# Two-layer hybrid encoder trunk on one core: which FFN blocks are computed by seven products, which chunks they pair, and where the norm factors live

## The chip, the cores and the metric

The kernel runs on one core of one Trainium2 chip. The core has five engines, each with its own list of instructions: TensorE (PE, matmuls, with the loading of its stationary operand shown apart as PEld), VectorE (DVE), ScalarE (ACT), GpSimd (POOL) and SyncE (SP), which here issues most DMA transfers; some others are issued by POOL. An instruction starts when its engine reaches it and the semaphores that it waits for have been raised. The metric is the device time of one launch in microseconds, the median of several runs.

## What is computed

Two layers over 512 tokens of width 1024 in float32: three token mixers whose outputs are gated and merged, an output projection, a SwiGLU FFN of inner width 2816, and a gated embedding; every sublayer starts with an RMS norm. Cut to what the change touches:

```python
def rmsnorm(x, g):
    x32 = x.astype(jnp.float32)
    y = x32 * lax.rsqrt(jnp.mean(x32 * x32, axis=-1, keepdims=True) + EPS)
    return (y * g.astype(jnp.float32)).astype(x.dtype)
...
    for i in range(DEPTH):
...
        merged = (ga * (ya @ w_br_a[i]) + gb * (yb @ w_br_b[i])
                  + gc * (yc @ w_br_c[i]))
        x = x + merged @ w_o[i]
        h = rmsnorm(x, norm_ffn[i])
        x = x + (jax.nn.silu(h @ w_ffn_gate[i]) * (h @ w_ffn_up[i])) @ w_ffn_down[i]
        h = rmsnorm(x, norm_ple[i])
        x = x + jax.nn.sigmoid(h @ w_ple_gate[i]) * (p[i] @ w_ple_in[i])
    return rmsnorm(x, norm_final)
```

## The kernel before

*Layout.* Activations lie transposed: the 1024 features are 8 chunks of 128 partitions, each chunk 512 tokens wide. The 2816 inner features are 22 blocks of 128. The host lays each weight out by blocks of 128 output features, [128, 1024], in which column group k holds the weights of input chunk k.

*Float32 from halves.* Each operand is split in two: `split` (line 161) makes a high half on ACT (L142, rounded to fp32r) and the rest, the low half, on DVE (L156). A product is three matmuls, high times high, high times low and low times high (`mm3`, L176 to L178). `weights` (line 165) loads a block of weights on SP's queue and splits it.

*Norms.* A norm's factor is a number for each token, so it is taken out of the product: `norm_chunk` puts h = x times gain into a tile and sums the squares; `norm` turns the sums by PE (L212), reduces them on DVE (L214), takes the root on POOL (L221), and spreads the factors over the partitions with four transposes (L225) whose result `spread` copies into a tile of tag "r". `rows` then sets `self.rb`, by which later results are multiplied. Work that needs it waits in `ready`.

*Order.* PE's list is written out by hand. For the other engines a scheduler places the instructions by priority; `weights` and the preparation within `seven` run at a priority raised by `w_ahead` = 400 places, and `behind` ties one instruction after another by hand. Tiles come from pools by tag: a tag with n buffers can hold n tiles, and a new tile waits until the last reader of the one that it replaces is done.

*The stages around the change, in one layer.* The differential stage (its rotary tables are two tiles of tag "r", its norm at about 249 us); the merge, in which chunk m of `merged` is accumulated in `gatec_x` and split into halves (`merge_b`, tiles `mergeb_y` and `mergeb_v`); the output projection `w_o` from about 456 us in the first layer, whose first two output chunks are a `pair` (line 193): chunks 0 to 6 of the input for both outputs, then chunk 7 for both; then `main_norm` and the FFN. The FFN goes in three parts (`PARTS`, blocks 0 to 7, 8 to 14, 15 to 21), each with its up and gate blocks and then a down projection.

*A block of the FFN.* The plain way: `gemm` (block 0: `pair`) for the gate and for the up product, 2 x 8 x 3 = 48 matmuls of 512 columns. The other way, `seven` (blocks 3 to 21): with input chunks j and j + 4 as rows and the two halves of the tokens as columns, the activations are 2 x 2 matrices b11, b12, b21, b22; the weights of the two products form a 2 x 2 matrix as well, and the four results come from seven products over four pairs j, thus 7 x 4 x 3 = 84 matmuls of 256 columns. The sums of the activations, t1 to t4 for each j, are made once a layer by `quarters` (line 909), two sets within `w_o` after chunks 5 and 6, two in the FFN after blocks 0 and 1. The sums of the weights, s1 to s4, are made for each block: s1 and s2 by a load on SP's queue and an accumulating DMA from POOL (L953) on top of it, s3 = s1 + a22 and s4 = s3 + a12 on DVE (L967, L971, which show as L156); a22 is loaded into a tile of tag "r" (`ffn_r`) and split into "kh" and "a". The tiles s1 to s4 lie in tag "qk" (`ffn_qk`).

Of the kernel before, what the change touches and what calls it, by code (L numbers as in the profile page):

```python
# [12 lines left out]
F32R = mybir.dt.float32r  # L13
# [7 lines left out]
P = 128  # L21
L = 2
# [3 lines left out]
D = 1024  # L26
KD = 8
# [11 lines left out]
NFB = DFF // P  # L39
# [9 lines left out]
BG = dict(glu=2, natten=1, values=3, diff=1, gatec=2, branchc=2, gateb=4, mergea=4, mergea2=2)  # L49
FIRST = (["v"] * 4 + ["pt"] * 2 + ["y", "b"], ["y"] * 5 + ["pt"] * 2 + ["b"])  # L50
EARLY = 6
SEVEN = tuple(range(3, 22))
GAP = 144
BACC = dict(dynamic_dma_scratch_size=1024)

# [5 lines left out]
class Net:  # L61
# [189 lines left out]
        self.run(self.norm(sq, D, waits, self.rows))  # L251

    def spread(self, bc):
        r = self.sb("r", [P, 512])
        self.act(r, bc, AF.Copy)
        return r

# [32 lines left out]
    def build(self):  # L290
        nc, tc, a = self.nc, self.tc, self.a
        self.bufs = dict(wr=3, wh=3, wl=3, h=8, qk=2, kh=2, v=4, pt=2, y=5, z=5, x=4, t=7, rp=4,
                         e=4, a=3, r=3, ss=1, sm=8, rc=4, b=2, s=8)
        self.bg, self.w_ahead = BG, 400
        self.pbufs = dict(mm=3, sc=2, tr=2, av=1)
        with tc.tile_pool(name="sb", bufs=1) as self.pool, \
                tc.tile_pool(name="ps", bufs=1, space=PSUM) as self.psum, \
                tc.tile_pool(name="dr", bufs=1, space=DRAM) as dram:
            xs = dram.tile([KD, P, 512], F32, name="xs")
            self.pis = dram.tile([KD, P, 512], F32, name="pis")  # L300
            with tc.manual_schedule(engines={mybir.EngineType.PE}):
                h = self.opening()
                xsrc = a["xT"]
                for i in range(L):
                    h = self.layer(i, h, xsrc, xs)
                    xsrc = xs
# [578 lines left out]
    def w_o(self, mg, xsrc):  # L885
        self.phase = "wo"
        xs, h, st, self.four = [], [], [], []
        for m in range(KD):
            if m % 2 == 0:
                two = self.parts_of("x", [512], 2)  # L890
            xo = two[m % 2]
            self.nc.sync.dma_start(xo, xsrc[m])
            if m == 0:
                both = [self.ps("mm") for _ in range(2)]
                self.pair(both, self.a["w_o"][self.i, 0:2], mg)
            if m < 2:
                ps = both[m]
            else:
                ps = self.ps("mm")
                self.gemm(ps, self.a["w_o"][self.i, m], mg)  # L900
            self.tt(xo, xo, ps, ALU.add)
            h.append(self.norm_chunk(m, xo, self.par(self.i, "ffn", m), "h", st))
            xs.append(xo)
            if m in (5, 6):
                self.four.append(self.quarters(xs, h, m - 5))
        self.main_norm(st[0])
        return xs, h

    def quarters(self, x, h, j):


        one, two = slice(0, 256), slice(256, 512)
        g = lambda k: self.par(self.i, "ffn", k)
        f = []
        for k in (j, j + 4):
            v = self.sb("t", [P, 512])
            self.act(v, x[k], AF.Copy, scale=g(k))
            f.append(v)
        b11, b12, b21, b22 = f[0][:, one], f[0][:, two], f[1][:, one], f[1][:, two]
        u = self.sb("t", [P, 2, 256])  # L920
        w = self.sb("t", [P, 2, 256])
        t1, t2, t3, t4 = u[:, 0], u[:, 1], w[:, 0], w[:, 1]
        self.tt(t1, b11, b12, ALU.subtract)
        self.tt(t2, b22, t1, ALU.add)
        self.tt(t3, b22, b12, ALU.subtract)
        self.tt(t4, t2, b21, ALU.subtract)
        if j < 2:
            d = [self.sb("rp" if n < 2 else "e", [P, 2, 256], F32R) for n in range(4)]
        else:
            d = [q for _ in range(2) for q in self.parts_of("v", [2, 256], 2, F32R)]  # L930
        for o, t in zip(d, (t1, t2, t3, t4)):
            self.split(o[:, 0], o[:, 1], t)
        ha, hb = self.halves(h[j]), self.halves(h[j + 4])
        cut = lambda p, c: (p[0][:, c], p[1][:, c])
        return dict(b11=cut(ha, one), b21=cut(hb, one), b22=cut(hb, two),
                    **{f"t{n + 1}": (o[:, 0], o[:, 1]) for n, o in enumerate(d)})
# [100 lines left out]
    def ffn(self, h, x):  # L1037
        self.phase = "ffn"
        i = self.i
        self.halfs, self.pending = 0, []  # L1040
        st, hn, bs = [], [], self.four
        spare = [[self.sb(t, [P, 1024], F32R) for _ in range(2)] for t in ("y", "pt")]
        self.sums, self.sevens = [t for _ in range(2) for t in self.parts_of("qk", [1024], 2)], 0
        for part in PARTS:
            mids = []
            for f, fb in enumerate(part):
                tags = (("mm", "mm", "mm"), ("sc", "sc", "av"))[fb % 2]
                md = self.sb("z" if f < 5 else "y", [P, 2, 512], F32R)
                mids.append(md)
                wg, wu = self.a["w_fg"][i, fb], self.a["w_fu"][i, fb]  # L1050
                if fb in SEVEN:
                    self.seven(wg, wu, bs, tags, spare[fb % 2], md, part[0] and f < 2)
                    continue
                g = self.sb("t", [P, 512])
                pg, pu = (self.ps(t) for t in tags[:2])
                if fb == 0:
                    self.pair((pg, pu), (wg, wu), h)
                else:
                    self.gemm(pg, wg, h)

                def gate(pg=pg, g=g):
                    self.tt(g, pg, self.rb, ALU.mult)
                    self.act(g, g, AF.Silu, table="silu")

                self.ready(gate)
                self.flush()
                if fb:
                    self.gemm(pu, wu, h)

                def up(pu=pu, g=g, md=md):  # L1070
                    self.tt(g, g, pu, ALU.mult)
                    self.split(md[:, 0, :], md[:, 1, :], g)

                self.ready(up)
                if fb in (0, 1):
                    self.four.append(self.quarters(x, h, 2 + fb))
            self.flush()
            down = [self.a["w_fd"][i, m][:, part[0] * P:(part[-1] + 1) * P] for m in range(KD)]
            two = [self.ps(("mm", "sc")[fb % 2 == 0]) for _ in range(2)]
            self.pair(two, down[:2], mids)  # L1080
            for m in range(KD):
                if m < 2:
                    ps = two[m]
                else:
                    ps = self.ps("mm")
                    self.gemm(ps, down[m], mids)
                d = self.sb("t", [P, 512])
                self.tt(d, ps, self.rb, ALU.mult)
                self.tt(x[m], x[m], d, ALU.add)
                if part is PARTS[-1]:  # L1090
                    if m in (0, 2):
                        qk = self.parts_of("qk", [2, 512], 2, F32R)
                    hn.append(self.norm_chunk(m, x[m], self.par(i, "ple", m),
                                              qk[m % 2] if m < 4 else "v", st))
        self.main_norm(st[0])
        return hn

# [189 lines left out]
        return None  # L1287


def _blocks(w):  # L1290
    k, m = w.shape[-2:]
    lead = w.shape[:-2]
    n = len(lead)
    w = w.reshape(*lead, k // P, P, m // P, P)
    w = w.transpose(*range(n), n + 2, n + 1, n, n + 3)
    return np.ascontiguousarray(w).reshape(*lead, m // P, P, (k // P) * P)
# [17 lines left out]
def _token_order():  # L1314
    t = np.arange(S)
    return (t % GR) * GW + t // GR
# [37 lines left out]
def _layout(v):  # L1354
    n = _token_order()
    f = {k: np.asarray(a) for k, a in v.items()}
    w_in = f["w_in"]
    par = []
    for i in range(L):
# [14 lines left out]
        "head": np.ascontiguousarray(np.concatenate([_cols(f["norm_mix"][0]), w_0[0, :, :P]], axis=1)),  # L1374
        "w_0": w_0,
        "w_in": _blocks(w_in),
        "w_va": _vblocks(w_in[:, :, OFF_VA:OFF_VA + 512]),
        "w_vc": _wide(w_in[:, :, OFF_VC:OFF_VC + 512]),
        "w_br_a": _blocks(f["w_br_a"]),
        "w_br_b": _blocks(f["w_br_b"]),  # L1380
        "w_br_c": _blocks(f["w_br_c"]),
        "w_o": _blocks(f["w_o"]),
        "w_fg": _blocks(f["w_ffn_gate"]),
        "w_fu": _blocks(f["w_ffn_up"]),
        "w_fd": _blocks(f["w_ffn_down"]),
        "w_pi": _blocks(f["w_ple_in"]),
        "w_pg": _blocks(f["w_ple_gate"]),
# [16 lines left out]
```

## Time and profile before

| what | value |
|---|---|
| median of 3 runs | 1789.35 us (1788.98 to 1789.88) |
| profiled execution, its own time | 1788.65 us |
| its span in the profile | 1786.9 us |
| mean granted TensorE clock | 0.999 |
| the first layer's FFN, 514 to 886 us: PE, DVE, ACT busy | 372.0, 281.5, 173.2 us |
| all DMA | 251.31 MB, 141 GB/s on the mean |

The span runs from the first to the last instruction that the profiler records; the time of an execution has about 1.75 us more around it. A page gives busy time by engine, a chain of waits followed back from the last instruction, and groups of instructions by line. An entry such as `L156 DVE TENSOR_TENSOR wo_x<-wo_x,wo_mm 128x512 f32<-128x512 f32 x2` is line 156 on DVE, writing a tile of tag "x" made in stage "wo". In a timeline the first two numbers are start and duration in us, and a bracket at the end gives the idle time ahead of the instruction and what ended it. Lines often are those of a helper, so a place is told by its tiles.

### The profile page before, as it was taken

What the parts mean: (1) busy time and instruction counts of PE and PEld (TensorE: products, weight loads), DVE (VectorE), ACT (ScalarE), POOL (GpSimd) and SP (SyncE); (2) the same over time, 40 slices, a digit from 0 to 9 for tenths busy, and PEclk for the clock granted to TensorE, in tenths of its full rate; (3) what the DMA queues carried; (4) which work ended last, traced back from release to release, by engine and by line L of the source; (5) the groups of instructions that cost most, each with busy time, mean ns of one, the idle gap of its engine ahead of it and who ended that gap; (6) DMA issues with size and microseconds to landing.
All of it is one profiled execution on the core that took longest, in us unless ns stands there. A gap on an engine that the chain in (4) does not pass through costs nothing.

```text
span 1786.9 us, 26874 instructions
## 1 busy us (share of the span) xinstructions
PE 1775.8 (99%) x9994; PEld 1554.5 (87%) x9994; DVE 1392.3 (78%) x2354; ACT 880.9 (49%) x1531; POOL 92.1 (5%) x134
## 2 busy tenths in 40 slices
PE   9999999999999999999999999999999999999998
PEld 7888888888889899998888888888888898989987
DVE  7877887997678587787776788889886775877776
ACT  5577555325465254454545765453355553534444
POOL 0000000000101011100000000000001010101000
PEclk9999999999999999999999999999999999999999
DMA  5666541334737366543447655323256473645332
GB/s 206 190 182 171 156 116 44 111 98 145 227 111 182 111 164 160 135 115 124 146 135 202 170 158 151 101 71 95 95 172 198 130 177 111 176 135 158 98 104 94
DMA packets 109907, 251.31 MB, mean 141 GB/s; under 512 B 14160, under 2 KB 18768, under 8 KB 109776
## 3 DMA queue, kind: packets, MB, share of 16 engines
q1 hardware_dynamic: 98112, 228.36, 41.6%
q0 software_dynamic: 10944, 19.93, 6.9%
q8 instruction: 79, 1.29, 0.3%
q10 hardware_dynamic: 720, 1.31, 0.2%
q14 instruction: 52, 0.43, 0.1%
HBM read 210.74 MB, written 7.34 MB: 122 GB/s over the span
## 4 chain that ended last, share of the span: by engine, by line
PE 96%; ACT 2%; DVE 1%; issue 0%; DMA 0%; POOLq 0%; DVEq 0%; ACTq 0%
PE ffn_mm L176 5%; PE ffn_mm L178 5%; PE ffn_mm L177 5%; PE ffn_mm L983 3%; PE ffn_mm L982 3%; PE ffn_mm L981 3%; PE ffn_sc L983 3%; PE ffn_sc L982 3%; PE ffn_sc L981 3%; PE mergea_mm L176 2%; PE mergea_mm L178 2%; PE mergea_mm L177 2%; PE diff_sc L783 2%; PE gatec_mm L176 2%; PE gatec_mm L177 2%; PE gatec_mm L178 2%
## 5 line engine op out<-in xcount | busy, mean ns | idle before, releaser
L159 DVE SCALAR_TENSOR_TENSOR conv_z<-glu_z,pre_par,conv_z 128x512 f32<-128x512 f32 x240 | 179.6, 748 | 3.3
L142 ACT ACTIVATE ffn_wh<-ffn_wr 128x1024 fp32r<-128x1024 f32 (+1 forms) x98 | 99.0, 1018 | 142.2 <-PE ffn_mm L177 103.5
L156 DVE TENSOR_TENSOR ffn_wl<-ffn_wr,ffn_wh 128x1024 fp32r<-128x1024 f32 (+1 forms) x98 | 114.7, 1177 | 15.8 <-ACT ffn_wh L142 15.1
L953 POOL DMA_DIRECT2D ffn_qk<-w_fu x76 | 67.4, 980 | 567.2 <-DMA ffn_qk<-w_fu 304.2
L156 DVE TENSOR_TENSOR ffn_t<-ffn_mm,wo_r 128x512 f32<-128x512 f32 (+1 forms) x66 | 40.6, 616 | 68.3 <-PE ffn_mm L178 68.3
L176 PE MATMUL ffn_mm<-ffn_z,ffn_wh 128*128 128x512 f32 x220 | 85.6, 389 | 0.0
L177 PE MATMUL ffn_mm<-ffn_z,ffn_wh 128*128 128x512 f32 x220 | 85.6, 389 | 0.0
L178 PE MATMUL ffn_mm<-ffn_z,ffn_wl 128*128 128x512 f32 x220 | 85.6, 389 | 0.0
L142 ACT ACTIVATE mergea_wh<-mergea_wr 128x1024 fp32r<-128x1024 f32 (+1 forms) x32 | 27.1, 846 | 96.8 <-PE mergea_mm L177 79.6
L142 ACT ACTIVATE ffn_wh<-ffn_qk 128x1024 fp32r<-128x1024 f32 x38 | 40.3, 1061 | 35.2 <-PE ffn_mm L177 17.1
L156 DVE TENSOR_TENSOR ffn_wl<-ffn_qk,ffn_wh 128x1024 fp32r<-128x1024 f32 x38 | 46.5, 1224 | 12.3 <-ACT ffn_wh L142 12.3
L156 DVE TENSOR_TENSOR ffn_t<-ffn_t,ffn_t 128x512 f32<-128x512 f32 (+1 forms) x50 | 30.8, 627 | 31.1 <-ACT ffn_t L142 30.3
L142 ACT ACTIVATE diff_a<-diff_sc,diff_s 128x512 f32<-128x512 f32 x32 | 22.0, 686 | 61.3 <-DVE diff_s L874 61.3
L178 PEld LDWEIGHTS ffn_mm<-ffn_z,ffn_wl 128*128 128x128 f32 x220 | 41.3, 188 | 8.6
L176 PEld LDWEIGHTS ffn_mm<-ffn_z,ffn_wh 128*128 128x128 f32 x220 | 41.3, 188 | 8.5
L177 PEld LDWEIGHTS ffn_mm<-ffn_z,ffn_wh 128*128 128x128 f32 x220 | 41.3, 188 | 8.4
L142 ACT ACTIVATE natten_wh<-natten_wr 128x1024 fp32r<-128x1024 f32 x24 | 25.4, 1058 | 41.5 <-PE natten_sc L650 14.2
L983 PE MATMUL ffn_sc<-wo_h,ffn_wl 128*128 128x256 f32 x160 | 45.3, 283 | 0.0
L982 PE MATMUL ffn_sc<-wo_h,ffn_wh 128*128 128x256 f32 x160 | 45.3, 283 | 0.0
L981 PE MATMUL ffn_sc<-wo_h,ffn_wh 128*128 128x256 f32 x160 | 45.3, 283 | 0.0
L874 DVE TENSOR_REDUCE diff_s<-diff_sc 128x1 f32<-128x512 f32 x64 | 42.1, 685 | 3.9 <-PE diff_sc L783 3.7
L983 PE MATMUL ffn_mm<-wo_h,ffn_wl 128*128 128x256 f32 x144 | 40.8, 283 | 0.0
(816 smaller groups left out, 6451.0 us busy)
## 6 DMA issues: line engine op xcount, KB each, us to landing
ffn_wr<-w_fg SPq DMA_DIRECT2D x44, 512.0 KB, 3.6
ffn_qk<-w_fu POOLq DMA_DIRECT2D x76, 256.0 KB, 5.6
ffn_wr<-w_fd SPq DMA_DIRECT2D x32, 448.0 KB, 3.8
ffn_qk<-w_fg SPq DMA_DIRECT2D x38, 256.0 KB, 3.9
ffn_qk<-w_fu SPq DMA_DIRECT2D x38, 256.0 KB, 4.3
ffn_r<-w_fu SPq DMA_DIRECT2D x38, 256.0 KB, 4.3
natten_wr<-w_in SPq DMA_DIRECT2D x16, 512.0 KB, 4.4
natten_b<-bias SPq DMA_DIRECT2D x32, 256.0 KB, 4.0
```

Of the source, the lines that this page charges most:

```text
L142: i = self.nc.scalar.activation(out, in_, func, **kw)
L156: return self.nc.vector.tensor_tensor(out, a, b, op)
L159: return self.nc.vector.scalar_tensor_tensor(out, a, s, b, op0, op1)
L176: mm(out, wh, ah, start=first, stop=False)
L177: mm(out, wh, al, start=False, stop=False)
L178: mm(out, wl, ah, start=False, stop=last)
L783: self.nc.tensor.matmul(out, st4[:, u, qs], st[:, ks], start=n == 0, stop=n == 1)
L874: nc.vector.tensor_reduce(out=m[:, u:u + 1], in_=sc, op=ALU.max, axis=AX.X, negate=True)
L953: nc.gpsimd.dma_start(q, wu[:, lo], accum_op=ALU.add)
L981: mm(out, wh[:, c], bh, start=first and k == 0, stop=False, skip_group_check=True)
L982: mm(out, wh[:, c], bl, start=False, stop=False, skip_group_check=True)
L983: mm(out, wl[:, c], bh, start=False, stop=k == 3, skip_group_check=True)
```

## The change

Five edits, all in effect together:

1. `SEVEN` is gone: in every layer all blocks but block 0 go by `seven`, blocks 1 and 2 too.
2. A pair is two neighbouring chunks, 2j and 2j + 1, where it was j and j + 4. Three sets of sums are made in `w_o`, after chunks 2, 4 and 6; the fourth stands in the FFN ahead of block 0's matmuls. The host orders the column groups of the gate and up weights to match (`_halves`), and block 0's pair takes the chunks in `ORDER`.
3. The sums of the third and fourth set lie in four "z" tiles taken at the start of `w_o`, where they lay in "v" tiles.
4. The FFN's eight mid tiles are taken once (four "v", one "z", three "y") where each part took up to five "z" and the rest "y"; the last four chunks of the next norm lie in "z" rather than "v".
5. The norm factors get tag "rb" with one buffer, and "r" goes from three buffers to two.

```diff
-SEVEN = tuple(range(3, 22))
+QUARTERS = (2, 4, 6)
+ORDER = (0, 2, 4, 6, 1, 3, 5, 7)
...
     def spread(self, bc):
-        r = self.sb("r", [P, 512])
+        r = self.sb("rb", [P, 512])
...
-                         e=4, a=3, r=3, ss=1, sm=8, rc=4, b=2, s=8)
+                         e=4, a=3, r=2, rb=1, ss=1, sm=8, rc=4, b=2, s=8)
...
     def w_o(self, mg, xsrc):
         self.phase = "wo"
         xs, h, st, self.four = [], [], [], []
+        self.zs = [self.parts_of("z", [2, 256], 2, F32R) for _ in range(4)]
...
-            if m in (5, 6):
-                self.four.append(self.quarters(xs, h, m - 5))
+            if m in QUARTERS:
+                self.four.append(self.quarters(xs, h, QUARTERS.index(m)))
...
-        for k in (j, j + 4):
+        for k in (2 * j, 2 * j + 1):
...
-            d = [q for _ in range(2) for q in self.parts_of("v", [2, 256], 2, F32R)]
+            d = [q for n in range(2) for q in self.zs[2 * j - 4 + n]]
...
-        ha, hb = self.halves(h[j]), self.halves(h[j + 4])
+        ha, hb = self.halves(h[2 * j]), self.halves(h[2 * j + 1])
...
+        md8 = [self.sb(t, [P, 2, 512], F32R) for t in ["v"] * 4 + ["z"] + ["y"] * 3]
...
-                md = self.sb("z" if f < 5 else "y", [P, 2, 512], F32R)
+                md = md8[f]
...
-                if fb in SEVEN:
+                if fb:
                     self.seven(wg, wu, bs, tags, spare[fb % 2], md, part[0] and f < 2)
                     continue
                 g = self.sb("t", [P, 512])
                 pg, pu = (self.ps(t) for t in tags[:2])
-                if fb == 0:
-                    self.pair((pg, pu), (wg, wu), h)
-                else:
-                    self.gemm(pg, wg, h)
+                for j in range(len(QUARTERS), 4):
+                    self.four.append(self.quarters(x, h, j))
+                self.pair((pg, pu), (wg, wu), [h[k] for k in ORDER])
...
-                self.flush()
-                if fb:
-                    self.gemm(pu, wu, h)
...
-                if fb in (0, 1):
-                    self.four.append(self.quarters(x, h, 2 + fb))
...
-                                              qk[m % 2] if m < 4 else "v", st))
+                                              qk[m % 2] if m < 4 else "z", st))
...
+def _halves(w):
+
+    b = _blocks(w).reshape(L, NFB, P, KD, P)
+    return np.ascontiguousarray(b[:, :, :, ORDER]).reshape(L, NFB, P, D)
...
-        "w_fg": _blocks(f["w_ffn_gate"]),
-        "w_fu": _blocks(f["w_ffn_up"]),
+        "w_fg": _halves(f["w_ffn_gate"]),
+        "w_fu": _halves(f["w_ffn_up"]),
```

## The prediction, made before the changed kernel ran

> **What bounds the kernel now.** I read the page's busy shares first, then its chain of waits, then busy time by stretch, and last the timeline at the places that the change touches.
>
> ```profile
> span 1786.9 us, 26874 instructions
> PE 1775.8 (99%) x9994; PEld 1554.5 (87%) x9994; DVE 1392.3 (78%) x2354; ACT 880.9 (49%) x1531; POOL 92.1 (5%) x134
> PE 96%; ACT 2%; DVE 1%; issue 0%; DMA 0%; POOLq 0%; DVEq 0%; ACTq 0%
> ```
>
> TensorE (PE) is busy 99% of the span and makes 96% of the chain that ended last. The time is therefore the length of the list of matmuls, plus every gap that an edit puts into it. The stretches of the first layer that matter, and one of sevens (770 to 780) for comparison:
>
> ```profile
> core 0: us, PE busy (x) PEld busy (x) DVE busy (x) ACT busy (x) POOL busy (x), PEclk, DMA share, GB/s
> 450.00:460.00 10.00, 10.00 (x46) 8.29 (x45) 8.33 (x11) 4.03 (x5) 1.94 (x2) 1.00 0.87 301
> 460.00:470.00 10.00, 10.00 (x46) 8.28 (x45) 5.57 (x7) 4.28 (x6) 2.15 (x3) 1.00 1.05 273
> 480.00:490.00 10.00, 10.00 (x46) 8.29 (x45) 6.30 (x9) 5.61 (x8) 0.00 (x0) 1.00 0.30 89
> 490.00:500.00 10.00, 10.00 (x46) 8.29 (x45) 10.00 (x23) 8.61 (x16) 0.00 (x0) 1.00 0.29 103
> 500.00:510.00 10.00, 10.00 (x49) 8.27 (x49) 3.20 (x6) 2.04 (x4) 1.03 (x1) 1.00 0.25 79
> 770.00:780.00 10.00, 10.00 (x86) 10.00 (x85) 8.94 (x16) 5.59 (x10) 0.00 (x0) 1.00 0.36 97
> ```
>
> PE is busy in all of them at a granted clock of 1.00. Two resources have no room in places: the DMA engines from 450 to 470 (0.87, then 1.05, which is all 16), and VectorE (DVE) from 490 to 500 and, nearly, within the sevens.
>
> **The change part by part.** *Blocks 1 and 2 by seven products.* In each layer two blocks of 48 matmuls of 512 columns become 84 matmuls of 256. The starts of block 2, of block 3 (the first seven now) and of block 4 are in the PE timeline:
>
> ```profile
> 520.06 0.39 PE L176 MATMUL ffn_mm<-wo_h,ffn_wh 128*128 128x512 f32 x1
> 530.71 0.39 PE L178 MATMUL ffn_mm<-wo_h,ffn_wl 128*128 128x512 f32 x1
> 530.94 0.28 PE L981 MATMUL ffn_sc<-wo_h,ffn_wh 128*128 128x256 f32 x1
> 541.01 0.28 PE L981 MATMUL ffn_mm<-wo_h,ffn_wh 128*128 128x256 f32 x1
> ```
>
> A plain block takes 530.94 - 520.06 = 10.88 us, a seven 541.01 - 530.94 = 10.07 us. (Per matmul that is 227 and 120 ns: 256 columns cost more than half of 512.) The saving is 0.81 us a block, and over four blocks 3.24 us. That is the whole gain the change can have, 0.18% of the time.
>
> *What the new sevens ask of others.* Each adds DVE and ScalarE (ACT) work; the stretch 770 to 780 shows that DVE at 8.94 of 10 still keeps PE busy. Its loads grow from 1.0 to 1.75 MB (512 KB and three times 256 KB on SP's queue, two accumulating ones of 256 KB on POOL's), under a DMA share of 0.25 to 0.30 between 480 and 510. I cost this at nothing; if DVE's 1.1 us of room in 10 were gone, each of four blocks would be late by what is missing.
>
> *Where the first seven's preparation lands.* This is the edit that matters. The preparation runs at raised priority, 400 places early, so with block 1 a seven it moves from block 2's time back into the output projection and beyond. In the built order of the changed program, VectorE's list at the start of that projection reads: accumulate merged chunk 7; then s3 = s1 + a22 of block 1, which waits for the first accumulating DMA of the stage (that which adds w_fu to s1); then the low half of merged chunk 7. Both layers have it. Before, that addition came first at 513.8:
>
> ```profile
> L156 DVE TENSOR_TENSOR ffn_qk<-ffn_qk,ffn_r x38: 684/687/690, 513.8 to 1673.3; 128x512 f32<-128x512 f32 x38
> ```
>
> and the stretch ran thus, with its counterpart in the second layer:
>
> ```profile
> 456.94 1.06 POOL L953 DMA_DIRECT2D ffn_qk<-w_fu  x1 [39.27 <-DMA wo_wr<-w_o]
> 456.95 0.69 DVE L156 TENSOR_TENSOR gatec_x<-gatec_x,gateb_v 128x512 f32<-128x512 f32 x1
> 458.34 0.69 DVE L156 TENSOR_TENSOR mergeb_v<-gatec_x,mergeb_v 128x512 fp32r<-128x512 f32 x1 [0.70 <-ACT mergeb_v L142]
> 463.33 0.39 PE L176 MATMUL wo_mm<-mergeb_v,wo_wh 128*128 128x512 f32 x1
> 463.55 0.39 PE L177 MATMUL wo_mm<-mergeb_v,wo_wh 128*128 128x512 f32 x1
> 464.21 1.37 DVE L156 TENSOR_TENSOR wo_x<-wo_x,wo_mm 128x512 f32<-128x512 f32 x2 [5.18 <-PE wo_mm L178]
> ...
> 1342.22 0.93 POOL L953 DMA_DIRECT2D ffn_qk<-w_fu  x1 [39.17 <-DVE wo_wl L156]
> 1348.93 0.39 PE L177 MATMUL wo_mm<-mergeb_v,wo_wh 128*128 128x512 f32 x1
> ```
>
> The low half of chunk 7 is made at 458.34, and PE first needs it at 463.55, in the second matmul of the pair's last chunk. There are 4.5 us of room, and DVE idles 5.18 us. Now the low half stands behind a DMA issued at 456.94. How long such a DMA takes, by the views of DMA issues over 456.5 to 457.2, over 1342 to 1342.5, over 458.3 to 458.9 (the stage's second), and over the whole span:
>
> ```profile
> ffn_qk<-w_fu POOLq DMA_DIRECT2D x1, 256.0 KB, 8.3
> ffn_qk<-w_fu POOLq DMA_DIRECT2D x1, 256.0 KB, 7.5
> ffn_qk<-w_fu POOLq DMA_DIRECT2D x1, 256.0 KB, 9.1
> ...
> ffn_qk<-w_fu POOLq DMA_DIRECT2D x76, 256.0 KB, 5.6
> ```
>
> First layer: it lands at 456.94 + 8.3 = 465.24; the addition holds DVE for 0.60 (456.35 to 456.95 is the step from one such operation to the next), the low half takes 0.69, so PE goes on at 466.53, 2.98 us late. Second layer: 1342.22 + 7.5 + 1.29 = 1351.01 against 1348.93, 2.08 us late. Together 5.06 us. The ends: with 5.6 us the waits are 0.28 and 0.18, with 9.1 us 3.78 and 3.68, so 0.46 to 7.46 us. I take the two rows themselves, because the queue ahead of that DMA hardly changes: in the built order the loads before it are the same up to 454, and then a load of 256 KB for block 2 takes the place of a residual load of 256 KB. Queued behind the waiting addition are the low half, then the residual additions of chunks 0 and 1, which wait for PE anyway; SP's queue stops too, since the load of block 3's a22 waits for the addition to free its buffer, but the residual and weight loads behind it are needed some 20 us later.
>
> A rule speaks to each half of this. The built order puts the addition ahead, and the Trainium skill, "TensorE: Matmul & The Clock Gate", section "Architectural detail: the array is 16× 32×32, not 1× 128×128", says that the queues of ACT and DVE are strictly first in, first out; no run here shows it yet, and if DVE could pass the addition by, the sum would lose its 5.06 us. The rows say 8.3 and 7.5 us for 256 KB; the Trainium skill, "DMA: Bandwidth & Descriptors", section "Anatomy of one DMA — SWDGE (gpsimd) path", fits 2.0 us plus bytes over 436,000 per us, an estimate of 2.6 us here; by that the DMA would land at 459.5, the wait would be nothing and the time 1786.1. Here the rows differ from the page, and I go by the rows.
>
> *Pairs of neighbouring chunks.* The number of sums is the same; three sets instead of two are made within the projection, the fourth at once after it. A set is eight DVE operations of 256 columns, 0.34 us apart, 2.7 us. The new first set, after chunk 4, falls into 480 to 490, where DVE has 3.7 us idle. The last set now stands ahead of the norm:
>
> ```profile
> L156 DVE TENSOR_TENSOR wo_t<-wo_t,wo_t x12: 422/426/429, 490.3 to 1382.4; 128x256 f32<-128x256 f32 x12
> ...
> 503.41 0.69 DVE L214 TENSOR_REDUCE wo_sm<-wo_tr 128x4 f32<-128x512 f32 x1 [1.99 <-PE wo_tr L212]
> 504.46 1.03 POOL L221 TENSOR_TENSOR wo_rc<-wo_sm,pre_power 128x4 f32<-128x4 f32 x1 [32.34 <-DVE wo_sm L217]
> 508.70 0.60 PE L225 MATMUL wo_tr<-pre_ident,wo_rc 128*128 128x128 f32 x4
> ```
>
> The norm's own factor is ready at 505.5 and needed at 508.70. DVE had 2 us idle ahead of the reduction, so 2.7 us more make it about 1 us late, and 2 us of room remain. Nothing.
>
> *A tile of their own for the norm factors.* It frees two buffers for a22 before the factors exist. So block 1's and block 2's a22 load right after the rotary tables' last use (the first table's last read is the DVE row), and ACT splits block 1's a22 ahead of the softmax work of the differential stage:
>
> ```profile
> 241.22 0.68 DVE L156 TENSOR_TENSOR diff_rp<-diff_rp,diff_r 128x512 f32<-128x512 f32 x1
> 245.00 1.04 ACT L142 ACTIVATE gatec_wh<-gatec_wr 128x1024 fp32r<-128x1024 f32 x1
> 247.09 0.59 ACT L142 ACTIVATE diff_ss<-diff_av 128x512 f32<-128x512 f32 x1
> 249.19 0.60 PE L212 MATMUL diff_tr<-pre_ident,diff_ss 128*128 128x128 f32 x4
> ...
> ffn_qk<-w_fg SPq DMA_DIRECT2D x1, 256.0 KB, 3.6
> ffn_r<-w_fu SPq DMA_DIRECT2D x38, 256.0 KB, 4.3
> ```
>
> Issued at 241.9 it lands at 245.5 (3.6 us) or 246.2 (4.3). The split takes 0.6, so what starts at 245.00 starts at 246.1 or 246.8. The squares then end at 248.8 or 249.5, against 249.19: nothing, or about 0.3 us a layer. I take nothing, and keep 0.6 for the range. The rotary tables are loaded earlier too, at places where the next load waits for a buffer; nothing.
>
> *The sum*, against the profiled execution: 1788.65 us, which is the span of 1786.9 and 1.75 around it. 1788.65 - 3.24 + 5.06 = 1790.47. The median of the runs, 1789.35, stands 0.70 above that execution, so the forecast is **1791.2 us**, 0.10% over the time before. From no change a measurement of this kernel can tell about 0.2%, 3.58 us, so this counts as no change.
>
> **The rivals.** *The wait is covered.* If the first accumulating DMA landed by 463.55 - 1.29 = 462.26 in the first layer, after 5.3 us, and after 5.4 in the second, the saving would be whole: 1789.35 - 3.24 = 1786.1. For it speaks the median of 5.6 us; against it the DMA share of 1.05 at just that place. It lies 0.3 us inside the bound of 0.2% (1785.8), and the three runs spread 0.9, so one time in four or so it would count as faster.
>
> *The wait is longer.* The loads of the first three sevens now follow each other without the residual loads between, and all share the 16 engines with the accumulating DMA. Price: 9.1 us in both layers, as the stage's second took, gives 7.46 - 3.24 = +4.22, or 1793.6; with 0.6 from the differential stage 1794.2. It decides the sign from waits of 3.24 + 3.58 = 6.82 us in sum, that is 0.9 us a layer more than the rows say. For it: the engines are full, and the second row of its kind took 9.1. Against: what stands ahead in the queue is the same.
>
> *The sevens run quicker than those seen.* At half of 227 ns a seven would take 9.5 us and the four save 5.4 us, and with a covered wait the time would be 1784.0. Against it: all of the seven quoted runs at 120 ns.
>
> **How the numbers follow.** Forecast 0.44, covered wait 0.18, longer wait 0.33, quicker sevens 0.05. Same takes the forecast and three quarters of the covered wait, 0.57; slower 0.33; faster 0.05 and a quarter of 0.18, 0.10. The range goes from 1785.7, which is the covered wait less the 0.4 us by which the quickest run lies under the median, to 1794.7, which is the upper bound of both unknown costs plus the 0.5 by which the slowest lies over it; left out are the quicker sevens and waits longer than any row shows.
>
> **What would show it.** Right: PE idle some 3 us and 2 us in the middle of the output projection's first pair, in both layers, put down to VectorE, with DVE's s3 addition ended by the accumulating DMA just before; blocks 1 and 2 at 10.07 us each. Wrong: no gap there (the DMA lands early, or the order on DVE doesn't hold), a gap at 249.19 or at 508.70 of the first layer, or sevens that leave PE idle in blocks 1 and 2.

## The result and the profile after

| | median | runs | from to |
|---|---|---|---|
| before | 1788.98 us | 15 | 1788.13 to 1789.88 |
| changed | 1793.96 us | 15 | 1789.47 to 1797.19 |

The ratio is 1.0028 (95% interval 1.002 to 1.0036): the changed kernel is slower by 0.28%, 5.0 us. Its runs also lie 7.7 us apart, where those of before lie 1.8 apart. The profiled execution took 1792.81 us, 4.16 more than that of before. From the page of the changed kernel, the span, the busy times and the chain by engine:

```profile
span 1791.0 us, 27255 instructions
PE 1774.5 (99%) x10138; PEld 1559.7 (87%) x10138; DVE 1410.6 (79%) x2394; ACT 891.6 (50%) x1551; POOL 99.3 (6%) x142
PE 91%; DVE 4%; DMA 2%; ACT 2%; issue 1%; SPq 0%; DVEq 0%; POOLq 0%; ACTq 0%
```

PE is busy for 1.3 us less than before and the span is 4.1 us longer, so time went into waiting; VectorE and DMA now have a share in the chain. The places where PE waits longest, in the view of waits (engine and line, what it waited for, us in total, times, longest):

```profile
PE wo_mm L178 <- DVE mergeb_v L157: 6.0, 2, 3.6
```

Two waits, one for each layer, at the output projection and for the tile of merged chunk 7. (Lines stand one or two further down than before: L176 to L178 are L177 to L179 now, L156 is L157.) VectorE's timeline of the first layer, then PE's:

```profile
456.99 0.69 DVE L157 TENSOR_TENSOR gatec_x<-gatec_x,gateb_v 128x512 f32<-128x512 f32 x1
465.96 0.69 DVE L157 TENSOR_TENSOR ffn_qk<-ffn_qk,ffn_r 128x512 f32<-128x512 f32 x1 [8.29 <-DMA ffn_qk<-w_fu]
466.57 0.69 DVE L157 TENSOR_TENSOR mergeb_v<-gatec_x,mergeb_v 128x512 fp32r<-128x512 f32 x1
...
463.37 0.39 PE L177 MATMUL wo_mm<-mergeb_v,wo_wh 128*128 128x512 f32 x1
467.31 0.50 PE L178 MATMUL wo_mm<-mergeb_v,wo_wh 128*128 128x512 f32 x1 [3.56 <-DVE mergeb_v L157]
467.65 0.39 PE L179 MATMUL wo_mm<-mergeb_v,wo_wl 128*128 128x512 f32 x1
```

The accumulate of chunk 7 is followed by the addition s3 (`ffn_qk<-ffn_qk,ffn_r`), which stands idle for 8.29 us until the accumulating DMA has landed, and the low half of chunk 7 comes behind it, at 466.57 instead of 458.34. The chain of waits through the same stretch ties the pieces together (start, duration, what):

```profile
457.27 8.67 DMA ffn_qk<-w_fu
465.94 0.02 issue
465.96 0.04 DVE ffn_qk L157
466.00 0.57 issue
466.57 0.70 DVE mergeb_v L157
```

The second layer has the same wait and something after it:

```profile
1350.15 0.39 PE L177 MATMUL wo_mm<-mergeb_v,wo_wh 128*128 128x512 f32 x1
1352.99 0.75 PE L178 MATMUL wo_mm<-mergeb_v,wo_wh 128*128 128x512 f32 x1 [2.46 <-DVE mergeb_v L157]
1353.55 0.63 PE L179 MATMUL wo_mm<-mergeb_v,wo_wl 128*128 128x512 f32 x1
1353.97 0.63 PE L177 MATMUL wo_mm<-mergeb_v,wo_wh 128*128 128x512 f32 x1
...
1356.52 0.39 PE L177 MATMUL wo_mm<-mergeb_y,wo_wh 128*128 128x512 f32 x1
1356.74 0.39 PE L178 MATMUL wo_mm<-mergeb_y,wo_wh 128*128 128x512 f32 x1
```

From 1353.0 to 1356.5 the matmuls start 0.43 us apart (1353.97 - 1353.55 = 0.42) instead of 0.227. The view by stretches says why; its columns are those shown in the prediction, and the granted clock is the third number from the end:

```profile
1349.00:1353.00 4.00, 1.54 (x8) 0.95 (x6) 1.29 (x2) 0.00 (x0) 0.88 (x1) 1.00 1.10 263
1353.00:1357.00 4.00, 4.00 (x11) 3.16 (x12) 2.19 (x3) 2.94 (x4) 1.73 (x2) 0.57 1.05 235
1357.00:1361.00 4.00, 4.00 (x19) 3.30 (x18) 3.38 (x5) 1.44 (x3) 0.00 (x0) 1.00 1.09 267
```

After the wait the clock stood at 0.57 over 4 us, so this gap cost more than its own length. Comparing the starts of equal matmuls in both traces gives the whole account of the span: +3.85 in the first output projection, -1.64 in the first FFN, -0.76 in the second layer's neighbourhood attention, +4.36 in the second output projection, -1.64 in the second FFN, in sum +4.17 against 4.16. The sevens did what they should. From PE's timeline, the starts of blocks 1, 2 and 3:

```profile
512.95 0.36 PE L983 MATMUL ffn_sc<-wo_h,ffn_wh 128*128 128x256 f32 x1
...
523.10 0.28 PE L983 MATMUL ffn_mm<-wo_h,ffn_wh 128*128 128x256 f32 x1
...
533.18 0.28 PE L983 MATMUL ffn_sc<-wo_h,ffn_wh 128*128 128x256 f32 x1
```

10.15 and 10.08 us, where a plain block took 10.88.

### The profile page after: what moved, and what is told of

It reads as the page before. It is cut to its first block, busy times and chain, and to the rows that moved or that the text cites. A ratio compares the mean times of both kernels' runs of the same rounds, so it can differ in the third digit from the quotient of the medians.

```text
span 1791.0 us, 27255 instructions
## 1 busy us (share of the span) xinstructions
PE 1774.5 (99%) x10138; PEld 1559.7 (87%) x10138; DVE 1410.6 (79%) x2394; ACT 891.6 (50%) x1551; POOL 99.3 (6%) x142
## 4 chain that ended last, share of the span: by engine, by line
PE 91%; DVE 4%; DMA 2%; ACT 2%; issue 1%; SPq 0%; DVEq 0%; POOLq 0%; ACTq 0%
PE ffn_mm L177 5%; PE ffn_mm L178 5%; PE ffn_mm L179 5%; PE ffn_mm L985 4%; PE ffn_mm L984 4%; PE ffn_mm L983 4%; PE ffn_sc L985 3%; PE ffn_sc L984 3%; PE ffn_sc L983 3%; PE mergea_mm L178 2%; PE mergea_mm L179 2%; PE mergea_mm L177 2%; PE diff_sc L784 2%; PE gatec_mm L177 2%; PE gatec_mm L178 2%; PE gatec_mm L179 2%
## 5 line engine op out<-in xcount | busy, mean ns | idle before, releaser
L157 DVE TENSOR_TENSOR ffn_wl<-ffn_wr,ffn_wh 128x1024 fp32r<-128x1024 f32 (+1 forms) x94 | 109.9, 1174 | 5.1 <-ACT ffn_wh L143 4.6
L955 POOL DMA_DIRECT2D ffn_qk<-w_fu x84 | 74.6, 996 | 550.5 <-DMA ffn_qk<-w_fu 218.1
L157 DVE TENSOR_TENSOR ffn_t<-ffn_mm,wo_rb 128x512 f32<-128x512 f32 (+1 forms) x66 | 40.0, 607 | 68.3 <-PE ffn_mm L179 68.3
L177 PE MATMUL ffn_mm<-ffn_v,ffn_wh 128*128 128x512 f32 x176 | 68.5, 389 | 0.0
L178 PE MATMUL ffn_mm<-ffn_v,ffn_wh 128*128 128x512 f32 x176 | 68.5, 389 | 0.0
L179 PE MATMUL ffn_mm<-ffn_v,ffn_wl 128*128 128x512 f32 x176 | 68.5, 389 | 0.0
L157 DVE TENSOR_TENSOR ffn_wl<-ffn_qk,ffn_wh 128x1024 fp32r<-128x1024 f32 x42 | 51.4, 1225 | 19.9 <-ACT ffn_wh L143 19.9
L157 DVE TENSOR_TENSOR ffn_t<-ffn_t,ffn_t 128x512 f32<-128x512 f32 (+1 forms) x48 | 31.4, 659 | 32.1 <-ACT ffn_t L143 31.5
L983 PE MATMUL ffn_sc<-wo_h,ffn_wh 128*128 128x256 f32 x176 | 50.0, 284 | 0.0
L985 PE MATMUL ffn_sc<-wo_h,ffn_wl 128*128 128x256 f32 x176 | 49.8, 283 | 0.0
L984 PE MATMUL ffn_sc<-wo_h,ffn_wh 128*128 128x256 f32 x176 | 49.8, 283 | 0.0
L984 PE MATMUL ffn_mm<-wo_h,ffn_wh 128*128 128x256 f32 x160 | 45.3, 283 | 0.0
L983 PE MATMUL ffn_mm<-wo_h,ffn_wh 128*128 128x256 f32 x160 | 45.3, 283 | 0.0
L143 ACT ACTIVATE ffn_kh<-ffn_r 128x512 fp32r<-128x512 f32 x42 | 26.6, 632 | 32.8 <-PE ffn_mm L984 16.2
```

The costliest lines, as they stand in the source:

```text
L143: i = self.nc.scalar.activation(out, in_, func, **kw)
L157: return self.nc.vector.tensor_tensor(out, a, b, op)
L177: mm(out, wh, ah, start=first, stop=False)
L178: mm(out, wh, al, start=False, stop=False)
L179: mm(out, wl, ah, start=False, stop=last)
L955: nc.gpsimd.dma_start(q, wu[:, lo], accum_op=ALU.add)
```

## The experiments

The theory was that the addition, put ahead of chunk 7's low half and waiting for a DMA, makes both gaps, and that the low clock follows from the gaps. The rivals: that the transfers themselves are late, so that the wait would show up elsewhere; that other edits cost time of their own; that the low clock has another cause. All ratios are against runs of the kernel before on the same chip (medians 1788.6 to 1788.7).

### The addition tied behind the low half

```diff
-            self.split(mg[:, 0, :], mg[:, 1, :], acc[m])
+            self.last = self.split(mg[:, 0, :], mg[:, 1, :], acc[m])
...
             self.behind(i, low)
+            if self.sevens == 1:
+                self.behind(i, self.last)
```

> The changed kernel with one tie more: the addition s3 of block 1 must come behind the low half of merged chunk 7 on VectorE. Theory (the addition, waiting for the accumulating DMA, holds up that low half, and TensorE with it): both gaps in the output projection go, with the slow matmuls behind the second one, and the saving of the four sevens (3.24 us) is left: 1789.0 - 3.2 = 1785.8 us, and runs as close together as those of before. Rival (the transfers of three sevens in a row are what is late, and the addition only shows it): the wait comes back further on, at the residual additions or the next weights, and the time stays at 1792 or more. The clock rival (the time is lost to the lower clock whatever the gap): about 1789.

1784.70 us (1784.22 to 1785.67), ratio 0.9977 (0.9969 to 0.9986): the forecast of 1785.8 was 1.1 too high, of which 0.6 is a shorter wait in the second layer that the last experiment looks at. VectorE's timeline at the place, and the two matmuls of PE between which the changed kernel has its gap:

```profile
457.64 0.69 DVE L157 TENSOR_TENSOR gatec_x<-gatec_x,gateb_v 128x512 f32<-128x512 f32 x1
459.03 0.69 DVE L157 TENSOR_TENSOR mergeb_v<-gatec_x,mergeb_v 128x512 fp32r<-128x512 f32 x1 [0.70 <-ACT mergeb_v L143]
466.26 0.69 DVE L157 TENSOR_TENSOR ffn_qk<-ffn_qk,ffn_r 128x512 f32<-128x512 f32 x1 [6.54 <-DMA ffn_qk<-w_fu]
466.87 1.28 DVE L157 TENSOR_TENSOR wo_x<-wo_x,wo_mm 128x512 f32<-128x512 f32 x2
...
464.02 0.39 PE L177 MATMUL wo_mm<-mergeb_v,wo_wh 128*128 128x512 f32 x1
464.24 0.39 PE L178 MATMUL wo_mm<-mergeb_v,wo_wh 128*128 128x512 f32 x1
```

The DMA is no quicker: the addition still runs at 466.26. But the low half is done 7 us earlier, and PE no longer waits there. The residual additions are late now, by some 2 us, and PE does not wait for them. So the gaps come from the order on VectorE, which makes PE wait for a transfer that it doesn't need there; the transfers are as long as before. One tie turns the change from a loss of 5.0 us into a gain of 4.0, so this kernel is faster than the one before and the changed one.

### Which edit puts the addition there

The prediction had it that block 1, as a seven, brings the addition forward. Two kernels part that from the fifth edit. First, the changed kernel with the norm factors back in tag "r":

```diff
-        r = self.sb("rb", [P, 512])
+        r = self.sb("r", [P, 512])
...
-                         e=4, a=3, r=2, rb=1, ss=1, sm=8, rc=4, b=2, s=8)
+                         e=4, a=3, r=3, ss=1, sm=8, rc=4, b=2, s=8)
```

> The changed kernel with the norm factors back in tag r with three buffers; blocks 1 and 2 stay sevens. In its built order the first s3 stands after block 0's first results, not ahead of chunk 7's low half. If the tile of its own is what moved the addition: no gap in the output projection, sevens at 10.07 us, 1785.8 us, or up to 2 us more, because block 1's a22 is now split just ahead of its use. If the blocks that became sevens are what moved it, as the prediction put it: the gaps stay, 1793 to 1795.

1795.38 us (1794.11 to 1796.48), ratio 1.0037 (1.0024 to 1.005). The output projection has no gap, so the first theory is right in that, and its time is wrong by nearly 10 us: another gap opened at block 1. ScalarE's timeline, then PE's:

```profile
509.99 0.58 ACT L143 ACTIVATE wo_r<-wo_tr 128x512 f32<-128x512 f32 x1
510.90 0.38 ACT L143 ACTIVATE ffn_t<-ffn_sc 128x256 f32<-128x256 f32 x1 [0.34 <-PE ffn_sc L985]
511.30 1.28 ACT L143 ACT_TABLE_LOAD   x1
512.60 0.63 ACT L143 ACTIVATE ffn_t<-ffn_t 128x512 f32<-128x512 f32 x1
513.13 1.14 ACT L143 ACTIVATE ffn_kh<-ffn_r 128x512 fp32r<-128x512 f32 x2
...
513.80 0.38 PE L983 MATMUL ffn_av<-wo_e,ffn_kh 128*128 128x256 f32 x1 [2.99 <-ACT ffn_kh L143]
```

The load of a22 was issued at 494.72 (at 242.62 in the tied kernel), and in this order its split comes behind the spreading of the norm factors, a table load of 1.28 us and block 0's Silu. It is done at about 513.7, and PE wanted it at 510.8. I had allowed for 2 us at most for both layers together; it is 3 in each, and the slow clock follows here too (0.63 from 513 to 517; in the second layer it lasts longer, as shown further down). So the fifth edit is what lets block 1 be a seven without a wait for a22, as the scheduler orders things; and it lets the addition, which needs a22 too, move up into the output projection.

Second, the kernel before with the fifth edit alone:

```diff
-        r = self.sb("r", [P, 512])
+        r = self.sb("rb", [P, 512])
...
-                         e=4, a=3, r=3, ss=1, sm=8, rc=4, b=2, s=8)
+                         e=4, a=3, r=2, rb=1, ss=1, sm=8, rc=4, b=2, s=8)
```

> The kernel before with the tile of its own for the norm factors alone (rb with one buffer, r with two); blocks 1 and 2 stay plain. If that edit alone moves the addition (block 3's s3 now) ahead of chunk 7's low half: gaps of 2.5 to 4 us in both layers as in the changed kernel, nothing saved, 1789.0 + 6.3 + the 1 to 2 us of slower matmuls = 1796 to 1798 us. If the prediction's cause (block 1 being a seven) is needed: no gap, 1789.0.

1797.78 us (1796.12 to 1798.55), ratio 1.0048 (1.0035 to 1.0061), as forecast for the case that this edit alone moves the addition. VectorE and PE in the first layer:

```profile
464.74 0.69 DVE L156 TENSOR_TENSOR ffn_qk<-ffn_qk,ffn_r 128x512 f32<-128x512 f32 x1 [7.21 <-DMA ffn_qk<-w_fu]
465.35 0.69 DVE L156 TENSOR_TENSOR mergeb_v<-gatec_x,mergeb_v 128x512 fp32r<-128x512 f32 x1
...
466.09 0.50 PE L177 MATMUL wo_mm<-mergeb_v,wo_wh 128*128 128x512 f32 x1 [2.48 <-DVE mergeb_v L156]
```

With blocks 1 and 2 plain, it is block 3's addition that stands ahead of the low half. The second layer waits 2.55 us at the same place and has slow matmuls behind the wait; the first has none. By the starts of equal matmuls the two places make some 7.2 of the 8.0 us by which this profiled execution is longer than that of before; the rest lies in the second layer's neighbourhood attention and isn't explained. So two lines about a buffer, in a kernel whose first seven runs 65 us later, are enough to make both gaps.

### The other edits, with the tie

Blocks 1 and 2 plain again in the kernel with the tie (edits 2 to 5 remain):

```diff
+PLAIN = (0, 1, 2)
...
-                if fb:
+                if fb not in PLAIN:
                     self.seven(wg, wu, bs, tags, spare[fb % 2], md, part[0] and f < 2)
                     continue
...
-                for j in range(len(QUARTERS), 4):
-                    self.four.append(self.quarters(x, h, j))
-                self.pair((pg, pu), (wg, wu), [h[k] for k in ORDER])
+                hp = [h[k] for k in ORDER]
+                if fb == 0:
+                    for j in range(len(QUARTERS), 4):
+                        self.four.append(self.quarters(x, h, j))
+                    self.pair((pg, pu), (wg, wu), hp)
+                else:
+                    self.gemm(pg, wg, hp)
...
+                self.flush()
+                if fb:
+                    self.gemm(pu, wu, hp)
```

> The kernel with the tie, with blocks 1 and 2 plain again: edits 2 to 5 and the tie without the four sevens. Theory (pairs, mid tiles and sums ahead of block 0 cost nothing): no gap in the output projection, blocks 1 and 2 at 10.88 us, and the time of before, 1788.7 us; or 1788.1 if the shorter wait in the second layer's neighbourhood stage comes with edits 2 to 4 and not with the sevens. Against the kernel with the tie (1784.7) the difference is the price of the four plain blocks, 3.3 to 4.0 us. Rival (the edits cost something that the sevens had to pay for): over 1789.5.

1788.37 us (1788.02 to 1790.51), ratio 1.0001 (0.9992 to 1.001). With the tie, edits 2 to 5 together cost nothing that can be measured (the interval is some 1.8 us to either side). The tied kernel, with the four sevens, is 3.7 us quicker than this one, nearly all of its gain of 4.0; of that, 0.6 is the shorter wait in the second layer that the last experiment looks at.

### What the slow matmuls come from

First, matmuls that fill the gap in the changed kernel (their result goes into a bank that nobody reads):

```diff
         for ks in (range(n - 1), (n - 1,)):
+            if fill and len(ks) == 1:
+                spare = self.ps("av")
+                for _ in range(fill):
+                    self.nc.tensor.matmul(spare, self.zero_r, self.halves(acts[0])[0], start=True, stop=True)
...
-                self.pair(both, self.a["w_o"][self.i, 0:2], mg)
+                self.pair(both, self.a["w_o"][self.i, 0:2], mg, fill=18)
```

> The changed kernel with 18 matmuls of 512 columns (zeros as weights, into a bank that nobody reads) in the output projection's first pair ahead of merged chunk 7, so that TensorE works where it idled: 18 x 0.227 = 4.1 us in each layer. They cover the gaps of 3.7 and 2.6 us. If the slower matmuls come from the idle time: no 0.43 us matmuls, granted clock 0.999 in every run, runs within 1.5 us of each other, and a time of 1785.8 + 8.2 = 1794.0 us, with up to 0.7 more where the wait is longer than the fill. If they come from something else (the DMA load, the time): the slow matmuls stay, the runs spread as those of the changed kernel do (1789 to 1797), and the median is 1795 or more.

1792.96 us (1792.12 to 1793.75), ratio 1.0023 (1.0014 to 1.0033). PE works 8.2 us more than it needs to, longer than it idled in the changed kernel's profile (6.0), and yet the time is no higher than the changed kernel's (1.0 us lower; the two intervals overlap), no 0.43 us matmul stands behind either place, the clock is 0.999 or 1.0 in all ten runs, and they lie 1.6 us apart instead of 7.7. Order and the waiting addition are as in the changed kernel, and the DMA share behind the place is 1.04 (467 to 471 us) with the clock at 1.00; only the idle time is gone. The fill also hides how long the wait is in each run, so the narrow spread alone doesn't tell the clock from the wait.

Second, idle time that waits for no DMA, in the kernel with the tie: VectorE makes the low half of chunk 7 n times more.

```diff
             self.last = self.split(mg[:, 0, :], mg[:, 1, :], acc[m])
+            for _ in range(8 if m == KD - 1 else 0):
+                self.last = self.tt(mg[:, 1, :], acc[m], mg[:, 0, :].bitcast(F32), ALU.subtract)
```

> The kernel with the tie, and VectorE makes the low half of merged chunk 7 nine times instead of once (eight more operations of about 0.73 us, the result the same), so that TensorE waits for VectorE at the same place, with no DMA in it. There were 4.6 us of room, so the gap is 8 x 0.73 - 4.6 = 1.2 us in each layer: 1784.7 + 2.4 = 1787.1 us. If idle time costs the clock only from a certain length on: no 0.43 us matmuls here, nothing on top. If any wait at this place does: up to 1.8 us more for each gap, 1790.7.

With n = 11:

> The same with eleven more operations: 11 x 0.73 - 4.6 = 3.4 us of idle time in each layer, about as long as the changed kernel's gaps. If idle TensorE is what lowers the clock: matmuls of 0.43 us behind some of the gaps, 0 to 1.8 us for each, different from run to run, thus 1784.7 + 6.8 = 1791.5 to 1795.1 us and runs that spread more than 2 us. If it is the DMA traffic or the waiting addition that lowers it: 1791.5 with runs as close together as with the tie (1.5 us) and a granted clock of 0.999 or more.

With n = 16:

> The same with sixteen more operations: 16 x 0.73 - 4.6 = 7.1 us of idle time in each layer. If idle time lowers the clock for a fixed time afterwards: slow matmuls behind both gaps in the profile, 1784.7 + 14.2 + 2 x 1.8 = 1802.5 us, runs close together again because every gap is long enough. If the price grows with the gap: 1806 or more. If idle time is not the cause: 1798.9.

| n | PE's wait, each layer | median | over the tied kernel | ratio to before |
|---|---|---|---|---|
| 8 | 1.2 us | 1787.72 us | 3.0 | 0.9995 (0.9986 to 1.0004) |
| 11 | 3.4 us | 1795.07 us | 10.4 | 1.0038 (1.0024 to 1.0052) |
| 16 | 7.0 us | 1803.57 us | 18.9 | 1.0082 (1.0069 to 1.0096) |

The waits are those of the view of waits; for n = 11 in PE's timeline:

```profile
466.94 0.50 PE L178 MATMUL wo_mm<-mergeb_v,wo_wh 128*128 128x512 f32 x1 [3.36 <-DVE mergeb_v L157]
467.27 0.40 PE L179 MATMUL wo_mm<-mergeb_v,wo_wl 128*128 128x512 f32 x1
...
468.46 0.63 PE L178 MATMUL wo_mm<-mergeb_y,wo_wh 128*128 128x512 f32 x1
468.89 0.63 PE L179 MATMUL wo_mm<-mergeb_y,wo_wl 128*128 128x512 f32 x1
...
471.84 0.39 PE L177 MATMUL wo_mm<-mergeb_y,wo_wh 128*128 128x512 f32 x1
```

1.2 us of idle time cost what they last, twice 1.2 and a little (3.0), with no slow matmul. Twice 3.4 cost 10.4, which is 3.6 more; twice 7.0 cost 18.9, 4.9 more. So idle time brings the slow matmuls, with the transfers that the tied kernel has too. Full DMA engines aren't needed for it: in the kernel with three "r" buffers the DMA share is 0.17 from 508 to 513 us, about the gap at block 1, and the clock falls behind it all the same.

The length of a wait does not decide alone. Waits of 2.46 us (the changed kernel, second layer) and 2.55 (the fifth edit alone, second layer) had slow matmuls behind them; waits of 2.48 (the fifth edit alone, first layer) and 3.56 (the changed kernel, first layer) had none, and what else decides isn't shown. Nor do the slow matmuls always last as long: 3.4 us here (471.84 - 468.46), 5.7 for n = 16 in the first layer (470.87 to 476.54), and 6.3 behind the wait of 2.99 us at block 1 in the second layer of the kernel with three "r" buffers, where they cost some 3 us on top of the wait. Its stretches there, with the clock as third number from the end:

```profile
1401.00:1405.00 4.00, 3.08 (x12) 2.78 (x13) 3.10 (x5) 2.40 (x5) 0.93 (x1) 0.57 0.38 53
1405.00:1409.00 4.00, 4.00 (x23) 4.00 (x22) 3.19 (x5) 1.85 (x4) 0.54 (x1) 0.58 0.81 277
```

For n = 16 in the first layer the stretches show that the clock fell while PE still stood:

```profile
460.00:465.00 5.00, 3.88 (x18) 2.87 (x16) 4.79 (x7) 0.00 (x0) 0.78 (x1) 1.00 1.01 242
465.00:470.00 5.00, 0.00 (x0) 0.00 (x0) 4.76 (x7) 0.00 (x0) 2.49 (x3) 0.62 1.12 228
470.00:475.00 5.00, 4.13 (x10) 3.27 (x11) 4.23 (x7) 3.21 (x4) 0.17 (x1) 0.50 0.92 205
```

For n = 11 the time lies at the upper end of what was expected: the price came in every one of the five runs (the lowest, 1794.42, is 9.7 over the tied kernel), and not in some of them. n = 8 lies 0.6 us and n = 16 1.1 us above what was expected, and the runs of n = 16 lie 2.2 us apart, not closer together than those with the tie (1.5).

### The kernel before once more

> The kernel before once more, for a second profile: in the first one a transpose of the second layer's neighbourhood stage waited 1.0 us for ScalarE (at 1046 us), where every kernel with blocks 1 and 2 as sevens waits 0.4. If that wait belongs to the kernel before: 0.9 to 1.1 us again, and the change gains some 0.7 us there besides the sevens. If it differs from run to run: 0.4 us, or another value, and no gain is put down to the change.

1788.54 us in one run. The transpose waited as long as in the first profile. From PE's timeline, this second profile of the kernel before and then the tied kernel:

```profile
1046.05 0.90 PE L708 MATMUL natten_tr<-pre_ident,natten_e 128*128 128x128 f32 x4 [1.00 <-ACT natten_e L142]
```

```profile
1044.47 0.90 PE L709 MATMUL natten_tr<-pre_ident,natten_e 128*128 128x128 f32 x4 [0.40 <-ACT natten_e L143]
```

The long wait stands in all four profiles with plain blocks 1 and 2 (before twice, the fifth edit alone, the tied kernel with plain blocks), and the short one in all with sevens. The difference is 0.6 us. Why the sevens of the first layer shorten it stays open: VectorE's list at that place is the same in the kernel before and in the changed one with three "r" buffers.

## Why the prediction came out as it did

The time, 1793.96 us, lies within the range (1785.7 to 1794.7) and on the side that the sum took, but the forecast of 1791.2 was 2.8 us too low and had the effect below what can be told from no change; it came out at 0.28%, more than the 0.2% set there, which was given a third of the chance. That the time still lies inside the range is partly luck: the upper end was made for a longer transfer, and what filled the room in the profiled execution was 1.28 us of longer waits and 1.74 of slow matmuls, for which the sum had no term. Against the profiled execution the sum was 1790.47 and the time 1792.81.

- *The saving.* 3.24 us forecast, 1.64 in each layer measured. Right, and the sevens of blocks 1 and 2 leave PE no wait.
- *The wait behind the addition.* Place, what PE waits for, and both layers as forecast: 2.98 and 2.08 us, against gaps of 3.72 and 2.62. The mis-sized terms are small: in the first layer the DMA was issued at 457.27, not 456.94, and landed after 8.7 us, not 8.3; in the second it was issued at 1344.07, which is 0.4 later than the 1342.22 moved on by the 1.45 us that the whole kernel had lost by then. The rows of before were the right measure, and VectorE did not pass the waiting addition by. The fit of the Trainium skill, "DMA: Bandwidth & Descriptors", section "Anatomy of one DMA — SWDGE (gpsimd) path", which makes 2.6 us of this transfer, does not hold for it here. From the view of DMA issues of the changed kernel, over 456.5 to 458.2 and over 1343 to 1345:

```profile
ffn_qk<-w_fu POOLq DMA_DIRECT2D x1, 256.0 KB, 8.7
...
ffn_qk<-w_fu POOLq DMA_DIRECT2D x1, 256.0 KB, 7.5
```

- *The step that failed in size* is "so PE goes on at 466.53, 2.98 us late", and the same for the second layer: it counts a stall at its own length. The second gap of 2.6 us cost 4.36, because the matmuls behind it ran at about half speed (0.43 us for 0.227). With the 1.74 us on top the sum is 1792.2; the longer waits (0.74 + 0.54), the first matmul after the wait (0.13) and the 0.76 won in the second layer bring it to 1792.9, against 1792.81. The median lies 1.15 above that execution; most runs show a granted clock of 0.997, the profiled one 0.998, but no trace shows where those runs lost the time. I left out the rule that speaks to it: the Trainium skill, "TensorE: Matmul & The Clock Gate", section "Part 1: The HAM clock gate (the "warmup" mystery)", says that TensorE falls to half its clock after an idle window of about 3.4 us and needs about as long of work to come back, by a window that runs on its own. The runs agree with half the clock (0.50 from 470 to 475 us for n = 16), and the shortest slow stretches with 3.4 us; the longest last 6.3. They differ in the threshold: a wait of 2.46 us was enough in the changed kernel's second layer, and one of 3.56 in its first had no slow matmul behind it.
- *The step that failed in its reason* is "so with block 1 a seven it moves from block 2's time back into the output projection". The tile of its own for the norm factors moves it, with or without block 1 as a seven, and that is the edit that the sum put at "I take nothing". The number was right because the built order had been read, not because the cause had been.
- *The rival "the wait is longer"* named 1793.6 and comes nearest, but for a reason that isn't the one measured: the DMA took 8.7 and 7.5 us, not 9.1, and the rest is clock.
- *Nothing* was right for the pairs, for the sums ahead of the norm (the spreading transposes begin at 512.59, which is 508.70 and the 3.89 us lost until then) and for the differential stage. Its split came as the shorter load said, and the turn of the squares stands at 249.23 against 249.19:

```profile
245.36 0.63 ACT L143 ACTIVATE ffn_kh<-ffn_r 128x512 fp32r<-128x512 f32 x1 [0.22 <-DMA ffn_r<-w_fu]
245.90 1.04 ACT L143 ACTIVATE gatec_wh<-gatec_wr 128x1024 fp32r<-128x1024 f32 x1
248.17 0.59 ACT L143 ACTIVATE diff_ss<-diff_av 128x512 f32<-128x512 f32 x1
```

- *Not foreseen at all:* 0.76 us won in the second layer's neighbourhood attention, of which 0.6 is the transpose above.

## What to carry to other kernels

A buffer that comes free earlier lets prepared work come earlier, and on an engine that takes its list in order, early work that waits for a DMA holds up everything behind it: after a change to pools or priorities, look in the built order for instructions whose semaphore is a DMA's, and at what stands behind them. The cure need not be to give the early start up; tying the waiting instruction behind the one urgent neighbour kept all of the gain here. And a gap of TensorE of 2.5 us or more is to be priced at its length and a range on top: behind the gaps of this case, 2.5 to 7 us long, the slow matmuls cost from nothing to about 3 us more.

## What the hardware showed that I had not expected

The clock can fall after TensorE is at work again: with n = 11 the matmuls kept 0.23 us for 1.5 us after the wait, and only then ran at 0.43 for 3.4 us. The changed kernel's 15 runs show granted clocks from 0.999 (1789.47 us) to 0.996 (1797.19 us): the same program, 7.7 us apart. The clock goes with the time, but it can't be the whole spread: the quickest run lies 1.6 us below the profiled execution less its 1.74 us of slow matmuls, so something else differs from run to run too. The first layer's transfer, which sets the wait, took from 7.6 to 8.7 us in the profiles of this case. Where such a spread appears with a lower mean clock and the kernel before has neither, a wait of TensorE some microseconds long is worth looking for.
